# Moving the last conditioning product into the entry of the feed-forward part, with results added by transfer and forms made later

## The chip, the cores and the metric

The kernel runs as one program on one core of a Trainium2 chip. The metric is the device time of one execution in microseconds. A matrix product on TensorE (PE in the profile) has a stationary operand, loaded by a weight load (PEld), and a moving one, whose columns stream through it; the result lands in PSUM, in banks of 512 fp32 columns by 128 partitions. VectorE (DVE) and ScalarE (ACT) read PSUM and work on SBUF, GpSimd (POOL) issues transfers of its own kind, and SyncE's queue (SP) issues the weight loads from HBM.

## What is computed

One decoder layer for 512 prompt rows and 8 sample rows (520 columns, with features on the partitions). Cut to what matters here:

```python
sh1, sc1, g1, sh2, sc2, g2 = ada_mod(c, w_ada, b_ada)     # six conditioning parts, each 2048 wide
...
merged = sigmoid(ga) * (y_m @ w_proj_a) + sigmoid(gb) * (y_f @ w_proj_b)
x = x + g1 * (merged @ w_out)
h2 = modulate(rmsnorm(x, norm2_w), sh2, sc2)
a, g = split(h2 @ w_ffn_in)                               # 2 x 5632 wide
f_out = (gelu(conv3(a) + conv_b) * g) @ w_ffn_out
x = x + g2 * f_out
```

`ada_mod` multiplies nine conditioning vectors (one of the prompt, eight of the samples) by `w_ada`, 2048 by 6 x 2048. So each of the six parts is a product with only nine rows of use, but 16.8 MB of weights. `g2`, the last of them, is needed only when `w_ffn_out` is multiplied.

## The kernel before, in words

**Products.** All large products keep fp32 accuracy with rounded operands: a weight is split into a rounded high part `wh` (a copy on ScalarE) and the rest `wl` (a subtraction on VectorE), as is the input, and each 128 x 128 block takes three matmuls, wh·xh, wh·xl and wl·xh (`three_of`). A matmul has 260 columns, half of the 520.

**Pairs.** From `w_out` on, two output rows of blocks at a time go through one step of Strassen's scheme: seven products instead of eight (`class Pair`, L256). A unit has seven products of 24 matmuls, numbered 1 to 7, in `ORDER` = (1,5,6,3,7,2,4), or for the first unit of a part `ORDER1` = (1,2,3,5,6,7,4) (L254). They go to the PSUM tiles `x` (products 1, 6, 7, 4), `y` (5, 3) and `z` (2). Product n needs its weights summed (`total`, tiles `sw`) and split (`split`), and the forms of the input `X[n]` (sums of the input's four quarters, each split in high and low part). `run_pairs` (L337) writes the order of work out by time steps t: at each step it finishes the product before (`take`), prepares weights two steps ahead (`ahead`), runs what the dictionary `late` holds for t, and issues product t.

**Order.** From L1139 to L1147 and from L1661 on, TensorE, VectorE and ScalarE keep the order in which the program lists their instructions (`Ordered`, L53). Weight tiles `raw` are 128 x 1024 (512 KB), in eight buffers (L157 to L163); SP issues their loads in program order, each as soon as a buffer is free.

**Conditioning.** `ada_mm` (L418) multiplies one block of 128 rows of `w_ada`: the stationary operand is `cs`, 128 x 32 (nine columns of use), and the 2048 outputs are four groups of 512 columns that go to four groups of 32 columns of the array (`tile_position=(0, 32*g)`), and so to four groups of 32 partitions of one bank `adp`. The operands are plain fp32, and each such matmul runs in two passes. The parts SC2 and SH2 are 18 steps (`ada_steps`, L503: eight of two blocks each and a last one, for each part) that `due` (L192) takes from a list at every `calls[2]`-th call. A dense product over 16 blocks calls `due` twice, one over eight blocks once. `calls` is (0, 1, 3) over the 16 dense products of the FoX projections (L1275), 1 of 5 over the last five gate products (L1444), and 1 of 2 over the products with `w_pb` (L1449). The part G2 has its own functions (L2104 to L2127): from the fourth unit of the feed-forward pairs on, one block is loaded into four `ar` tiles (`g2_load`) and multiplied before a product 2 (`g2_product`), 16 times, every second unit; then come a copy to SBUF, four transposes and the bias.

**The products with `w_pb`** (L1598 to L1636). 16 products over eight blocks. Product n of the loop has output block j of `order` = 0, 8, 1, 9, ..., 7, 15. It is multiplied by its gate in `mg[j]`, then the branch of `w_pa`, which lies in HBM (`dmg`) and was loaded into `mgo` by SP, is added on VectorE. Right after, `m_first` (j < 8) makes form 1 or `m_forms` makes the other six forms of blocks j-8 and j. Forms 6 and 4 of the blocks 0 to 6 go to HBM and are fetched back by POOL.

**The entry of the feed-forward part** (L1821 to L1884). The input `h2` comes half by half (`features`, VectorE and ScalarE, with the tiles `xa` and `bf`), and meanwhile the first three output blocks f = 0, 1, 2 are multiplied without Strassen's scheme, `eight(f, o, e, zs, w)`: eight blocks of K, one or two halves z, 24 matmuls for each half (`beside` takes two such sets side by side). Their PSUM tiles are `acc[f][o][z]`. For f = 1 these are four banks of their own, `fb`, of which 260 of 512 columns are used. `sums_of` and `sum_parts` make the forms for the pairs, `whole_conv` and `whole_gate` finish a block. The last set, `eight(2, 1, 1)`, is issued at step -2 of the pairs (L2136), and steps -1 to 3 hold what is left of the entry on VectorE.

Of the kernel before, what the change touches and what calls it, by code (L numbers as in the profile page):

```python
# [63 lines left out]
def tile_hybrid_step(ctx: ExitStack, tc: tile.TileContext, I, O):  # L64
# [28 lines left out]
    def pt(name, dt=F32):  # L93
        return sp.tile([P, 528], dt, tag="p", name=nm(name), bufs=8)
# [1177 lines left out]
        return t  # L1272

    pending += ada_steps(SC2) + ada_steps(SH2)
    calls[:] = 0, 1, 3  # L1275

    dqf = dram([2, NS, 4 * P], "dqf")
    sc = mconst([P, NPG, NS, FH], "sc")
# [190 lines left out]
    def m_forms(i):  # L1469

        a, b = mg[i], mg[8 + i]
        mX[2][i], mX[3][i] = hl_parts(hp, "hl", b)
        b11, b12, b21, b22 = (t[:, o:o + HN] for t in (a, b) for o in (0, HN))
        V.tensor_tensor(b11, b11, b12, op=ALU.subtract)
        V.tensor_tensor(b12, b22, b12, op=ALU.subtract)
        V.scalar_tensor_tensor(b22, b22, -1.0, b11, op0=ALU.mult, op1=ALU.subtract)
        V.scalar_tensor_tensor(b21, b22, -1.0, b21, op0=ALU.mult, op1=ALU.subtract)
        mX[5][i], mX[7][i] = hl_parts(hp, "hl", a)
        for n, f in ((6, b22), (4, b21)):
            t = (st if i == 7 else pt)("mf", F32R)  # L1480
            hi, lo = mX[n][i] = parts_of(t)
            S.copy(hi, f)
            V.tensor_tensor(lo, f, hi.bitcast(F32), op=ALU.subtract)
            if i < 7:
                G.dma_start(dxf[i + 8 * (n == 4)][:, :N], t[:, :N])
        mg[i] = mg[8 + i] = None
# [52 lines left out]
    class WoPair(AddPair):  # L1539
# [45 lines left out]
        def end(self, step):  # L1585

            if step == 0:
                self.add(1, 0, self.x)
            if step == 1:
                super().c11()  # L1590
                self.done(0)
                self.done(1)

# [3 lines left out]
    for n, j in enumerate(order):  # L1597
# [16 lines left out]
            units[0].load((1, 0), (1, 1))  # L1614
        if n % 2 == 0 and n // 2 + 2 < NB2:
            fetch_gate(n // 2 + 2)
        old = pt("mgo")
        nc.sync.dma_start(old[:, :N], dmg[j])
        acc = dense(I["w_pb"][j], yf, "pb", raw=early.pop(j, None))
        if n == KC - 1:  # L1620
            more.append(cf)
# [8 lines left out]
        V.tensor_tensor(mg[j][:, :N], mg[j][:, :N], old[:, :N], op=ALU.add)  # L1630
        if j < 8:
            m_first(j)
        else:
            m_forms(j - 8)
    yf = old = None

    def shift(c):
# [18 lines left out]
    def parts2(u, o, e):  # L1656
        return wtwo([raws.pop((u, o, e))], 1024)
# [34 lines left out]
    def first_weights(o):  # L1692
# [2 lines left out]

    r2 = st("rr")
    run_pairs(units, 2, {
        9: log_exp, 50: lambda: fetch_xa(range(8)), 51: lambda: (load2(0, 0, 0), load2(0, 1, 0)), 53: tot_parts,
        54: lambda: (first_weights(0), half_squares(1)), 55: lambda: (first_weights(1), half_norm(1))}, 0)
    mX = units = None  # L1700

# [73 lines left out]
    done = []  # L1775
    part = {}

    def whole_conv(f):
        at = new_at()
        for z in range(2):  # L1780
            S.copy(at[:, 2 + z * HN:2 + (z + 1) * HN], acc[f][0][z])
        acc[f][0] = None
        part[f] = conv_start(f, at)
        conv_end(f, at, part[f])

# [18 lines left out]
    def sum_parts(n):  # L1804
        src = [{5: xa[i][:, :HN], 7: xa[i][:, HN:N], 4: xa[8 + i][:, :HN], 6: xa[8 + i][:, HN:N]}[n] for i in range(8)]
        for j in range(8 + 1):
# [7 lines left out]
            if j >= 1:  # L1814
# [3 lines left out]
                else:  # L1818
                    V.tensor_tensor(lo, src[j - 1], hi.bitcast(F32), op=ALU.subtract)

    features(0, 1, {0: lambda: W2.end(0), 2: lambda: W2.end(1), 3: lambda: half_squares(0), 6: lambda: ws.append(parts2(1, 0, 0))})  # L1821
    load2(0, 0, 1)
    some = [(0, 0, ws[0]), (0, 1, ws[1])]
    beside(some, 0, 1, range(4))
    half_norm(0)
    acc.append([[mm_ps("fb")[:, :HN] for z in range(2)] for o in range(2)])
# [12 lines left out]
    for e in range(2):  # L1839
# [27 lines left out]
    eight(2, 1, 0, (1, 0), w0)  # L1867
    for i in range(8):
        hb.pop((i, 1))
    w = parts2(1, 1, 1)  # L1870
# [6 lines left out]
    for i in range(6, 8):  # L1877
        sums_of(i)
    eight(2, 0, 1, (0, 1), w0)
    w = parts2(2, 1, 1)  # L1880
    sum_parts(5)
    whole_gate(1)
# [216 lines left out]
        return late  # L2099


    box = {}

    def g2_load(k):  # L2104
        box["raw"] = [pt("ar") for _ in range(4)]
        for g, t in enumerate(box["raw"]):
            nc.sync.dma_start(t[:, :512], I["w_ada"][k * P:(k + 1) * P, G2 * DM + g * 512:G2 * DM + (g + 1) * 512])

    def g2_product(k):
        if k == 0:  # L2110
            box["ps"] = mm_ps("adp")
        ada_mm(box["ps"], [(k, t[:, :512], k == 0, k == KC - 1) for t in box.pop("raw")], False)

    def g2_out():
        box["sb"] = pt("ads")
        S.copy(box["sb"][:, :512], box.pop("ps"))

    def g2_turn():
        t = ada_turn(box.pop("sb"), 4)
        c0 = G2 * 16  # L2120
        dst = ada[:, c0:c0 + 16, :].rearrange("p (g j) i -> p j g i", g=4)
        bias = wide(C_ADA + c0, 16).rearrange("p (g j) i -> p j g i", g=4)
        for j in range(4):
            V.tensor_tensor(dst[:, j], t[:, j, :, :9], bias[:, j], op=ALU.add)
        negative(G2)

    g2 = {}  # L2127
    for k in range(KC):
        g2.update({7 * (4 + 2 * k) + 2: on(g2_load, k), 7 * (4 + 2 * k) + 5: on(g2_product, k)})
    g2.update({7 * 36: g2_out, 7 * 36 + 2: g2_turn})  # L2130
# [111 lines left out]
```

## Time and profile before

| | |
|---|---|
| median of 3 runs | 2923.01 us (2921.05 to 2929.48) |
| the profiled execution | 2912.86 us |
| its span, first to last instruction | 2911.2 us |
| mean granted TensorE clock | 0.997 |

The profile is of one execution. Times in its rows are microseconds from the start of the span. PE's rows give a modelled duration that is longer than the distance between the starts of two matmuls, since they overlap; the distance is what a matmul costs in a full stream. DMA share is the mean busy share of the core's 16 DMA engines. A row of the timeline merges instructions alike that follow each other; xN is their number, and what stands in brackets is the engine's idle time before, and what ended it.

### The profile page before, as it was taken

The numbers are of one execution on the slowest core, as the hardware profiler recorded it, in microseconds if no ns is written. First come the engines' busy times: TensorE is split into PE (matmuls) and PEld (weight loads), VectorE is DVE, ScalarE is ACT, GpSimd is POOL, SyncE is SP. The second block draws the span as 40 slices with busy tenths as digits, with TensorE's granted clock in tenths as the row PEclk, the third lists the DMA queues.
The fourth block names the chain that finished last, engine by engine and source line by source line (L and its number), as shares of the span: only waits on it lengthen the run. The fifth ranks groups of instructions, "written<-read, shape, count | busy, mean of one in ns | idle before, by whom it ended". The sixth has DMA issues, their size and how long they took to land. (4 is left out here: it accounts for less than half of the span.)

```text
span 2911.2 us, 58503 instructions
## 1 busy us (share of the span) xinstructions
PE 2853.6 (98%) x23460; PEld 2730.7 (94%) x23460; DVE 2176.0 (75%) x3984; ACT 1341.4 (46%) x2321; POOL 419.6 (14%) x681
## 2 busy tenths in 40 slices
PE   6999999999999999999999999999999999999999
PEld 4889998999999889889999999999999999999999
DVE  4777875577864567358888888888888888787787
ACT  3234433355544545334555544444444445544543
POOL 0003430211110122501111100000000001100100
PEclk9999999999999999999999999999999999999999
DMA  9933437845445555787672344344434436746752
GB/s 338 305 115 114 149 125 268 293 153 168 146 152 172 196 176 189 247 302 247 208 245 73 122 137 153 126 148 136 154 128 146 138 124 182 193 157 188 203 160 89
DMA packets 214138, 514.16 MB, mean 177 GB/s; under 512 B 24481, under 2 KB 77073, under 8 KB 213865
## 3 DMA queue, kind: packets, MB, share of 16 engines
q1 hardware_dynamic: 177072, 416.01, 43.9%
q0 software_dynamic: 36352, 94.18, 10.7%
q8 instruction: 184, 3.01, 0.4%
q14 instruction: 90, 0.73, 0.1%
q10 hardware_dynamic: 440, 0.23, 0.0%
HBM read 440.40 MB, written 66.46 MB: 174 GB/s over the span
## 5 line engine op out<-in xcount | busy, mean ns | idle before, releaser
L60 ACT CAST wh<-sw 128x512 fp32r<-128x512 f32 x640 | 366.7, 621 | 244.9 <-PE z L60 87.2
L60 PE MATMUL x<-bf,wh 128*128 128x260 f32 x2624 | 476.9, 283 | 1.0 <-DVE tg L60 0.5
L60 DVE TENSOR_TENSOR wl<-sw,wh 128x512 fp32r<-128x512 f32 x640 | 412.3, 686 | 83.2 <-ACT wh L60 80.3
L60 DVE TENSOR_TENSOR wl<-raw,wh 128x1024 fp32r<-128x1024 f32 (+2 forms) x325 | 337.7, 1051 | 121.2 <-ACT wh L60 115.2
L60 ACT CAST wh<-raw 128x1024 fp32r<-128x1024 f32 (+2 forms) x325 | 292.0, 912 | 268.6 <-PE x L60 122.7
L60 PEld LDWEIGHTS x<-bf,wh 128*128 128x128 f32 x2624 | 404.1, 188 | 1.4 <-DVE tg L60 0.7
L60 PE MATMUL x<-bf,wl 128*128 128x260 f32 x1312 | 369.8, 282 | 0.0
L178 DVE TENSOR_TENSOR wl<-raw,wh 128x1024 fp32r<-128x1024 f32 (+1 forms) x140 | 171.5, 1226 | 194.5 <-ACT wh L177 180.9
L177 ACT CAST wh<-raw 128x1024 fp32r<-128x1024 f32 (+1 forms) x140 | 144.1, 1031 | 285.1 <-issue 50.5
L60 PEld LDWEIGHTS x<-bf,wl 128*128 128x128 f32 x1312 | 246.6, 188 | 0.0
L60 PE MATMUL y<-bf,wh 128*128 128x260 f32 x1312 | 239.2, 283 | 2.9 <-ACT wh L60 2.4
L60 PEld LDWEIGHTS y<-bf,wh 128*128 128x128 f32 x1312 | 201.4, 188 | 3.3 <-ACT wh L60 2.6
L60 DVE TENSOR_TENSOR sw<-raw,raw 128x512 f32<-128x512 f32 x316 | 203.1, 683 | 0.0
L60 PE MATMUL x<-ff,wh 128*128 128x260 f32 x1024 | 186.3, 283 | 0.0
L60 PE MATMUL y<-bf,wl 128*128 128x260 f32 x656 | 185.0, 282 | 0.2 <-DVE wl L60 0.2
L60 PEld LDWEIGHTS x<-ff,wh 128*128 128x128 f32 x1024 | 157.9, 188 | 0.0
L60 PE MATMUL x<-ff,wl 128*128 128x260 f32 x512 | 144.6, 282 | 0.0
L60 PE MATMUL x<-hf,wh 128*128 128x260 f32 x720 | 131.6, 282 | 1.0 <-ACT wh L60 0.6
L60 PE MATMUL fo<-fe,wh 128*128 128x260 f32 x768 | 125.4, 284 | 1.1 <-DVE fo L60 0.9
L60 PEld LDWEIGHTS y<-bf,wl 128*128 128x128 f32 x656 | 123.4, 188 | 0.4 <-DVE wl L60 0.4
L60 PE MATMUL z<-bf,wh 128*128 128x260 f32 x656 | 121.6, 286 | 0.0
L60 PEld LDWEIGHTS z<-bf,wh 128*128 128x128 f32 x656 | 100.8, 188 | 13.4 <-issue 13.4
(597 smaller groups left out, 7607.0 us busy)
## 6 DMA issues: line engine op xcount, KB each, us to landing
raw<-in_w_fi SPq DMA_DIRECT2D x176, 512.0 KB
raw<-in_w_in SPq DMA_DIRECT2D x156, 512.0 KB
ar<-in_w_ada SPq DMA_DIRECT2D x192, 256.0 KB
raw<-in_w_ada SPq DMA_DIRECT2D x96, 512.0 KB
raw<-in_w_fo SPq DMA_DIRECT2D x64, 512.0 KB
raw<-in_w_out SPq DMA_DIRECT2D x32, 512.0 KB
raw<-in_w_fo SPq DMA_DIRECT2D x32, 384.0 KB
dff<-cc POOLq DMA_DIRECT2D x44, 260.0 KB
```

The costliest lines, as they stand in the source:

```text
L60: return lambda *a, **k: self.tc.keep_in_program_order(getattr(self.eng, op)(*a, **k))
L177: S.copy(wh[:, o], t[:, :m])
L178: V.tensor_tensor(wl[:, o], t[:, :m], wh[:, o].bitcast(F32), op=ALU.subtract)
```

## The change

1. `calls` over the FoX projections is (0, 1, 2) in place of (0, 1, 3): a step of SC2 and SH2 at every second call.
2. In the loop over `w_pb`, for the first 14 products the branch of `w_pa` is no longer loaded by SP and added by VectorE: POOL issues a transfer from HBM that adds it to `mg[j]`. The last two keep the old way. The forms of product n are made at the end of product n+1. At the end of the last one stand `m_first(7)` and the first part of `m_forms(7)`, now called `m_second`; the rest of `m_forms(7)` comes at step 0 of the pairs with `w_out`.
3. The tiles x, y and z of the last `w_out` unit are let go at its end.
4. G2 moves from the pairs into the entry. Its eight double steps (two blocks each, loaded as four `raw` tiles of 512 KB) stand between the sets of the entry. Its four groups of 512 columns are cut in three pieces of 252, 252 and 8 columns, which go to the spare columns 260 to 511 of three of the four `fb` banks. A group's three pieces follow each other. The copy to SBUF takes three instructions; transposes, bias and `negative` (`g2_turn`) stand after `eight(2, 0, 1)`.
5. At the start of the pairs, `whole_conv(2)` is split: its copies from PSUM stay at step -1, the rest goes to step 1; `sum_parts(7)` moves from step -1 to 2, `whole_gate(2)` from 0 to 3, `sum_parts(4)` from 3 to 4.

```diff
-    calls[:] = 0, 1, 3
+    calls[:] = 0, 1, 2
...
-        old = pt("mgo")
-        nc.sync.dma_start(old[:, :N], dmg[j])
+        if n >= KC - 2:
+            old = pt("mgo")
+            nc.sync.dma_start(old[:, :N], dmg[j])
...
-        V.tensor_tensor(mg[j][:, :N], mg[j][:, :N], old[:, :N], op=ALU.add)
-        if j < 8:
-            m_first(j)
+        if n < KC - 2:
+            G.dma_start(mg[j][:, :N], dmg[j], accum_op=ALU.add)
         else:
-            m_forms(j - 8)
+            V.tensor_tensor(mg[j][:, :N], mg[j][:, :N], old[:, :N], op=ALU.add)
+        for i in order[n - 1:n] + order[n:] * (n == KC - 1):
+            if i < 8:
+                m_first(i)
+            elif i < KC - 1:
+                m_forms(i - 8)
+            else:
+                m_second(7)
...
+    def g2_load(k):
+        box["raw"] = [[wraw(I["w_ada"][i * P:(i + 1) * P, G2 * DM + e * 1024:G2 * DM + (e + 1) * 1024])
+                       for e in range(2)] for i in (k, k + 1)]
+
+    def g2_room():
+        (_, a), (b, c) = fbt[1], fbt[0]
+        return [(c, 0, 252), (b, 252, 504), (a, 504, 512)]
+
+    def g2_product(k):
+        for i, t in zip((k, k + 1), box.pop("raw")):
+            for g in range(4):
+                for bank, a, b in g2_room():
+                    T.matmul(bank[32 * g:32 * g + 32, HN:HN + b - a], cs[:, i, :],
+                             t[g // 2][:, g % 2 * 512 + a:g % 2 * 512 + b], start=False, stop=(i == KC - 1),
+                             tile_position=(0, 32 * g), skip_group_check=True)
+        if k < KC - 2:
+            g2_load(k + 2)
...
     beside(some, 0, 0)
+    g2_load(0)
     eight(1, 0, 0, (0,), ws[2])
...
     eight(1, 1, 0, (1, 0), w)
+    g2_product(0)
...
     features(1, 1, {3: lambda: some.append((0, 1, parts2(0, 1, 1)))})
     load2(2, 0, 0)
+    g2_product(2)
     beside(some, 1, 1)
...
     features(1, 0)
+    g2_product(4)
     beside(some, 1, 0)
+    g2_product(6)
...
     whole_conv(0)
     w0 = parts2(2, 0, 0)
     load2(1, 1, 1)
+    g2_product(8)
     eight(1, 0, 1, (0, 1), w)
...
+    g2_product(10)
     eight(2, 0, 0, (1, 0), w0)
...
+    g2_product(12)
     eight(2, 1, 0, (1, 0), w0)
+    g2_product(14)
+    g2_out()
...
     eight(2, 0, 1, (0, 1), w0)
+    g2_turn()
     w = parts2(2, 1, 1)
     sum_parts(5)
     whole_gate(1)
...
-    run_pairs(units, 2, {-2: lambda: eight(2, 1, 1, (0, 1), w), -1: lambda: (whole_conv(2), sum_parts(7)),
-                         0: lambda: whole_gate(2), 3: lambda: sum_parts(4),
-                         **g2, **whole[0].begin(7 * len(units))})
+    run_pairs(units, 2, {-2: lambda: eight(2, 1, 1, (0, 1), w), -1: lambda: whole_copy(2),
+                         1: lambda: whole_conv(2), 2: lambda: sum_parts(7), 3: lambda: whole_gate(2),
+                         4: lambda: sum_parts(4),
+                         **whole[0].begin(7 * len(units))})
```

More of the change, by code (lines that the diff above doesn't have):

```diff
@@ L1467, in m_first, with m_second, m_forms @@
         V.tensor_tensor(lo, a[:, :HN], hi.bitcast(F32), op=ALU.subtract)
-    def m_forms(i):
+    def m_second(i):
+        mX[2][i], mX[3][i] = hl_parts(hp, "hl", mg[8 + i])
+    def m_forms(i, second=True):
         a, b = mg[i], mg[8 + i]
-        mX[2][i], mX[3][i] = hl_parts(hp, "hl", b)
+        if second:
+            m_second(i)
         b11, b12, b21, b22 = (t[:, o:o + HN] for t in (a, b) for o in (0, HN))
@@ L1590, in end @@
                 super().c11()
+                self.x = self.y = self.z = None
                 self.done(0)
@@ L1697, in tile_hybrid_step @@
     run_pairs(units, 2, {
-        9: log_exp, 50: lambda: fetch_xa(range(8)), 51: lambda: (load2(0, 0, 0), load2(0, 1, 0)), 53: tot_parts,
+        0: lambda: m_forms(7, False), 9: log_exp, 50: lambda: fetch_xa(range(8)), 51: lambda: (load2(0, 0, 0), load2(0, 1, 0)), 53: tot_parts,
         54: lambda: (first_weights(0), half_squares(1)), 55: lambda: (first_weights(1), half_norm(1))}, 0)
@@ L1776, in tile_hybrid_step, with whole_copy @@
     part = {}
-    def whole_conv(f):
-        at = new_at()
+    def whole_copy(f):
+        part[f] = at = new_at()
         for z in range(2):
@@ L1782, in whole_conv @@
         acc[f][0] = None
+    def whole_conv(f):
+        if f not in part:
+            whole_copy(f)
+        at = part[f]
         part[f] = conv_start(f, at)
@@ L1819, in sum_parts, with g2_out, g2_turn @@
                     V.tensor_tensor(lo, src[j - 1], hi.bitcast(F32), op=ALU.subtract)
+    box = {}
+    def g2_load(k):
[13 more added lines that the diff above has]
+            g2_load(k + 2)
+    def g2_out():
+        box["sb"] = pt("ads")
+        for bank, a, b in g2_room():
+            S.copy(box["sb"][:, a:b], bank[:, HN:HN + b - a])
+    def g2_turn():
+        t = ada_turn(box.pop("sb"), 4)
+        c0 = G2 * 16
+        dst = ada[:, c0:c0 + 16, :].rearrange("p (g j) i -> p j g i", g=4)
+        bias = wide(C_ADA + c0, 16).rearrange("p (g j) i -> p j g i", g=4)
+        for j in range(4):
+            V.tensor_tensor(dst[:, j], t[:, j, :, :9], bias[:, j], op=ALU.add)
+        negative(G2)
     features(0, 1, {0: lambda: W2.end(0), 2: lambda: W2.end(1), 3: lambda: half_squares(0), 6: lambda: ws.append(parts2(1, 0, 0))})
@@ L1825, in tile_hybrid_step @@
     half_norm(0)
-    acc.append([[mm_ps("fb")[:, :HN] for z in range(2)] for o in range(2)])
+    fbt = [[mm_ps("fb") for z in range(2)] for o in range(2)]
+    acc.append([[t[:, :HN] for t in ts] for ts in fbt])
     beside(some, 0, 1, range(4, 8))
@@ L1866, in tile_hybrid_step @@
         sums_of(i)
+    g2_product(12)
     eight(2, 1, 0, (1, 0), w0)
+    g2_product(14)
+    g2_out()
+    fbt = None
     for i in range(8):
@@ L2099, in rest_of @@
         return late
[L2102 to L2130, printed above, removed]
     units = [FfnPair(f, ORDER1 if f == 3 else ORDER) for f in range(3, KF)]
```

## The prediction

> **What bounds the kernel.** First the page: TensorE is busy for 98% of the span, at full clock nearly everywhere.
>
> ```profile
> span 2911.2 us, 58503 instructions
> PE 2853.6 (98%) x23460; PEld 2730.7 (94%) x23460; DVE 2176.0 (75%) x3984; ACT 1341.4 (46%) x2321; POOL 419.6 (14%) x681
> ```
>
> So the change can only win where PE waits, or where work leaves PE. Second, the chain in order of time, in the pairs, where the G2 product (`adp`) is now:
>
> ```profile
> 1653.83 2.89 PE z L60 x24
> ...
> 1673.94 2.88 PE z L60 x24
> ...
> 1694.07 0.99 PE adp L60 x8
> 1695.06 3.07 PE z L60 x24
> ...
> 1715.37 2.89 PE z L60 x24
> ```
>
> The chain runs on PE alone. A product takes 2.88 us for 24 matmuls, 0.12 each. A unit without G2 takes 1673.94 - 1653.83 = 20.11; the next two units take 1715.37 - 1673.94 = 41.43, not 40.22. One G2 block thus costs 1.21 (0.99, and the rest around it), and its 16 blocks 16 x 1.21 = **19.4 us**, uncovered.
>
> Third, the stretches around the entry, cut where sets of products begin. (Columns: length, busy time of PE, PEld, DVE, ACT, POOL, granted clock, DMA share, GB/s.)
>
> ```profile
> 1519.30:1526.10 6.80, 6.18 (x25) 5.79 (x25) 5.26 (x12) 3.71 (x8) 2.04 (x6) 0.50 0.73 270
> 1551.70:1553.60 1.90, 0.90 (x5) 0.50 (x4) 1.90 (x7) 1.31 (x3) 0.00 (x0) 1.00 0.37 65
> 1553.60:1593.60 40.00, 40.00 (x335) 40.00 (x335) 37.17 (x80) 23.63 (x48) 7.99 (x11) 1.00 0.26 91
> 1593.60:1616.20 22.60, 18.53 (x147) 17.50 (x146) 22.27 (x46) 11.25 (x25) 5.90 (x7) 1.00 0.33 106
> ```
>
> The entry is nearly as tight on VectorE (37.17 of 40, then 22.27 of 22.6) as on PE. PE loses about 1.5 us in the second row, where it waits for features. In the last row it does six products, 17.3 us of work, in 22.5: 5.2 lost. About 1.9 of those are three places where one tile is used by two products in a row (3 then 5, 6 then 7, 7 then 4, some 0.63 each); 3.3 are VectorE being late. DMA is light, 91 GB/s.
>
> **Part by part.**
>
> *G2 out of the pairs:* -19.4, worked out above. The four transposes cost the same 0.5 in either place.
>
> *G2 in the entry.* The trace has the same double step, with 512 columns whole, for another conditioning part:
>
> ```profile
> 436.45 0.40 PE L223 MATMUL gate<-hh,wl 128*128 128x260 f32 x2
> 436.79 1.92 PE L421 MATMUL adp<-raw,cs 128*32 128x512 f32 x16
> 438.64 0.51 PE L223 MATMUL gate<-hh,wh 128*128 128x260 f32 x2
> 438.99 0.40 PE L223 MATMUL gate<-hl,wh 128*128 128x260 f32 x2
> ```
>
> From 436.45 to 438.99 less four ordinary matmuls (0.48) is 2.06 us for two blocks, against 2.42 for two single ones: each return to full-width matmuls costs some 0.36. Eight double steps are 16.5; two pairs of them (0 and 2, 6 and 8) stand with no product between, so -0.7. The pieces of 8 columns add 2 passes in each of 16 blocks, four groups abreast: 32 passes that the trace doesn't show, between 0 and the 0.12 of a 260-column matmul, 0 to 3.8. I take 0.04 (far nearer to empty), 1.3. Sum **+17.1**, if the four groups still run abreast. That is the open point (first two rows: `adp`'s instructions alone that lie in a stretch of 0.03 us, on PE, PEld and ACT):
>
> ```profile
> 1693.99:1694.02 0.03, 0.02 (x4) 0.03 (x4) 0.00 (x0) 1.00 1.01 416
> 1694.44:1694.48 0.04, 0.04 (x8) 0.00 (x0) 0.00 (x0) 1.00 0.50 208
> 1694.00 1.06 PE L60 MATMUL adp<-ar,cs 128*32 128x512 f32 x8
> L60 PE MATMUL adp<-ar,cs x128: 592/605/617, 1694.0 to 2315.8; 128*32 128x512 f32 x128
> ```
>
> Four passes begin within 0.03 us, one of each group, and the second four about 0.45 later: eight passes of 0.6 each end within 1.06. The program lists a group's two passes one after the other, so a group doesn't hold up the next one for at least one waiting pass. After the change five passes of group 0 are listed ahead of group 1. If they hold it up, a block takes four times one group's time: 4 x (4 passes of 252 columns at 0.215 + 2 x 0.04) = 3.8 instead of about 1.0, **+45** over 16 blocks. Between "abreast" and that lies everything; I take abreast, since every group of passes seen overlaps fully.
>
> The Trainium skill ("TensorE: Matmul & The Clock Gate", Part 3) says that matmuls start and end strictly in program order. By that rule the +45 would hold. The rows above contradict it for the passes, as the second pass of one group starts after the first of the next, but they can't exclude it for whole matmuls. The same page gives the queue 64 entries; the 36 weight loads and passes listed ahead of the last group would fit.
>
> *Its loads.* G2 adds 32 loads of 512 KB to the eight `raw` buffers. SP is already waiting for free buffers there:
>
> ```profile
> SPq L163 <- DVE wl L60: 32.6, 5, 14.2
> 1240.00:1310.00 70.00, 70.00 (x582) 61.69 (x575) 40.63 (x72) 21.40 (x36) 4.32 (x8) 1.00 0.90 312
> ```
>
> The second row shows what the transfers can give: 312 GB/s at a share of 0.90, so 347. Counting buffers in program order, the loads for steps 0 and 2 are in before PE reaches them at 1551.7. All later ones wait for buffers that step 0 frees. From its half to the second half of step 8 there are 15 loads (12 of G2, 3 of `w_fi`), 7.9 MB or 22.7 us, and I add 2 from issue to first bytes (an estimate, 0 to 4). PE's own work in that time is two sets of 5.8 and 4 double steps, 19.6. So PE waits **+5.1** (3 to 7), most of it at steps 4 and 8, which have nothing or one set in front. If the groups run one after the other this wait vanishes. Behind the waiting step on PE stand the entry's sets, and what VectorE makes from them.
>
> *What it covers:* the 1.5 us of waiting for features, **-1.5**.
>
> *The new tie of VectorE to PE.* `g2_turn` puts four VectorE additions, in program order, ahead of the last weights' split and of `sum_parts(5)`; they read transposes that follow `eight(2, 0, 1)` on PE. Until now VectorE ran ahead here:
>
> ```profile
> 1584.02 1.22 DVE L60 TENSOR_TENSOR wl<-raw,wh 128x1024 fp32r<-128x1024 f32 x1
> 1585.15 2.80 DVE L60 TENSOR_TENSOR bf<-xa,bf 128x260 fp32r<-128x260 f32 x8
> 1587.87 0.75 DVE L60 TENSOR_TENSOR cc<-fb,cc 128x260 f32<-128x260 f32 x2
> 1588.54 2.79 DVE L60 SCALAR_TENSOR_TENSOR bf<-xa,bf 128x260 fp32r<-128x260 f32 x8
> 1591.26 1.28 DVE L60 TENSOR_TENSOR sw<-raw,raw 128x512 f32<-128x512 f32 x2
> 1592.46 1.21 DVE L60 TENSOR_TENSOR wl<-raw,wh 128x1024 fp32r<-128x1024 f32 x1
> 1593.60 1.28 DVE L60 TENSOR_TENSOR sw<-sw,raw 128x512 f32<-128x512 f32 x2
> L60 DVE TENSOR_TENSOR ada<-adq,sv x4: 179/180/185, 2350.4 to 2350.7; 128x36 f32<-128x36 f32 x4
> ```
>
> `eight(2, 1, 1)` is the last 5.8 us before 1593.6, so PE ended `eight(2, 0, 1)` at about 1587.8; the split (first row) was done by 1585.2. Now VectorE can begin only when the transposes are through: four additions of 0.18, the negation, 1.22 for the split, about 2.3 us in which PE has two matmuls to do: wait 2.3. From the split's end VectorE needs 1593.60 - 1585.15 = 8.45 until product 1 has its weights; PE has 5.5: wait 3.0. Moving `whole_conv(2)` and `sum_parts(7)` behind then lets products 2, 3 and 5 go through, but the same VectorE work remains before product 4 and the next unit: 1.3 more, and the 1.9 of the tile uses. Together 8.5 in place of 5.2, **+3.3** (0 to +6). The lead that VectorE gains while PE does G2 is lost at this tie.
>
> *Waits and the clock.* A lowered clock cost 3.4 us once (first stretch row: 6.8 us at 0.50). The 2.4 us wait for product 3 (1593.60:1616.20) left it at 1.00. So I take 0, and 3.4 more as the upper end. The Trainium skill ("TensorE: Matmul & The Clock Gate", Part 1) has the clock halve after an idle window of about 3.4 us; by that rule a wait of 3.0 could do it or not, which would add the same 3.4.
>
> *Results added by transfer, forms later.* VectorE drops 14 additions:
>
> ```profile
> L1630 DVE TENSOR_TENSOR sgm<-sgm,mgo x16: 690/700/701, 1253.4 to 1350.9; 128x520 f32<-128x520 f32 x16
> L1563 POOL DMA_DIRECT2D tot<-sq x13: 887/902/964, 1376.9 to 1499.7; - x13
> 1355.19 0.28 PE L60 MATMUL z<-mf,wl 128*128 128x260 f32 x1
> 1356.65 0.51 PE L60 MATMUL y<-mf,wh 128*128 128x260 f32 x2 [1.19 <-ACT wh L60]
> ```
>
> That is 9.8 us, but VectorE is busy for only 40.6 of 70 us there (row 1240:1310), so it is worth nothing in the loop. POOL's adding transfers take about 0.9 to issue and have a whole product, 5.8 us, to land before the form reads `mg[j]`; they cover themselves. At the end of the loop the order changes: product 3 of `w_out` waited 1.35 us (last two rows) behind `m_forms(7)`; now that comes after its weights, but before product 5's, and one more form (of block 6) has slid to the last product. What product 5 waits on is nearly the same sum. I take **-0.7** (-2 to +1). Letting x, y, z go earlier: nothing waits on them. The rate of SC2 and SH2: 32 calls at 1 of 2 make 16 steps instead of 10, and the last 2 of 18 follow in the gates, so none is left for the `w_pb` loop. The same steps at 2.06 us cost PE the same earlier; the loop's DMA share of 0.90 shows that PE (70.00 of 70) bears a denser stream: 0 (-1 to +2).
>
> **Sum:** -19.4 + 17.1 + 5.1 - 1.5 + 3.3 - 0.7 = **+3.9** on the profiled execution, 2912.9 to 2916.8. That execution is 10 us below the median of the three runs, 2923.0; on the median's scale, 2927.
>
> **Rivals.**
>
> *A, groups one after the other* (slower). Place: `g2_product`. Price: +45, less the load waits of 5.1, so +44 in all: 2967. It decides from the point where the queue in front of a group's passes holds fewer than the five that the others must jump. For it: the order of the program; against: the rows at 1694. A milder form, in which a group starts when the one before is half through, gives about 2.2 a block: +20 - 5 + 4 = +19, 2942.
>
> *B, PE fills VectorE's gaps* (faster). If buffers come free sooner than I count (no load waits) and VectorE catches up after its tie (no loss at the boundary): 3.9 - 5.1 - 3.3 = -4.5, 2918.5; with the lowered clock at 1519 gone as well, -8, 2915. For it: PE gets 17 us more work in the entry, in which VectorE's stays the same. Against: VectorE's order is fixed.
>
> *C, the change doesn't do what it says:* the forms spread nothing, since the last product now carries three of them: product 5 waits 1 to 2 us longer, 2929. Inside the range.
>
> **Chances.** Forecast (abreast, loads and tie as priced) 0.5, with a range of its own of 2919 to 2935; A's mild form 0.2, A in full 0.17; B 0.13. The range leaves out the lower part of B and the upper part of A: 2917 to 2964. A measurement of this kernel can tell about 0.3% (8.8 us) from no change. Faster by that needs more than all of B: 0.06. Within it: most of B and about seven tenths of the forecast, 0.43. Slower: A and the rest, 0.51.
>
> **What would show it.** The `adp` passes' place: one double step of about 2.2 us (abreast) or 7 (one after another) between sets. PE waiting on `raw` from `w_ada` before steps 4 and 8. VectorE idle until the transposes, then PE waiting for `wl` at `eight(2, 1, 1)` and product 1. A unit of the pairs at 20.11 throughout. The forecast is wrong if G2's passes take much over 1.1 us a block, or if PE's waits between the entry and the steady pairs come to less than 8 or more than 20.

## The result, and the profile after

The changed kernel is slower: 2968.2 us median (2964.5 to 2971.4, four runs) against 2922.0 (2920.6 to 2929.5) before, a ratio of 1.0154 (95% interval 1.0138 to 1.0170). The profiled execution took 2964.5 us, 51.6 more than that of before. The page of the changed kernel begins so:

```profile
span 2962.8 us, 58873 instructions
...
PE 2882.9 (97%) x23716; PEld 2763.4 (93%) x23716; DVE 2166.8 (73%) x3970; ACT 1340.6 (45%) x2323; POOL 423.1 (14%) x695
```

TensorE is busy 29 us longer, and the span is 52 us longer: so part is work (or slower work), part is waiting. Where it lies is seen when both traces are cut at the same matmuls. First before, then after, in four stretches: the FoX projections (first to last matmul on `fi`), the products with `w_pb`, from their end to the first matmul of the entry (the pairs with `w_out`), and the entry. (Columns: length, busy time of PE, PEld, DVE, ACT, POOL, granted clock, DMA share, GB/s.)

```profile
868.90:1126.20 257.30, 254.24 (x2021) 230.62 (x2021) 150.53 (x343) 128.66 (x250) 43.16 (x42) 1.00 0.54 182
...
1246.75:1349.42 102.67, 102.67 (x853) 94.81 (x852) 71.18 (x122) 35.88 (x55) 8.07 (x16) 1.00 0.83 284
1349.42:1517.39 167.97, 163.70 (x1353) 162.34 (x1352) 140.98 (x269) 90.86 (x150) 33.97 (x54) 1.00 0.75 233
1517.39:1593.54 76.15, 74.25 (x581) 72.86 (x582) 65.21 (x144) 43.54 (x84) 13.32 (x29) 0.96 0.32 108
```

```profile
870.32:1133.74 263.42, 263.42 (x2127) 233.96 (x2127) 151.86 (x346) 129.66 (x252) 43.02 (x44) 1.00 0.67 227
...
1256.20:1370.33 114.13, 100.22 (x769) 97.14 (x768) 52.48 (x87) 31.03 (x49) 19.87 (x27) 0.96 0.59 155
1370.33:1546.81 176.48, 167.29 (x1354) 165.49 (x1352) 148.53 (x283) 93.59 (x156) 34.87 (x56) 0.98 0.73 223
1546.81:1661.12 114.31, 109.26 (x970) 95.68 (x970) 63.17 (x145) 40.77 (x79) 10.48 (x29) 0.97 0.63 219
```

| stretch | before | after | difference |
|---|---|---|---|
| FoX projections | 257.3 | 263.4 | +6.1 |
| from there to the first product with `w_pb` | 120.6 | 122.5 | +1.9 |
| products with `w_pb` | 102.7 | 114.1 | +11.5 |
| pairs with `w_out`, up to the entry | 168.0 | 176.5 | +8.5 |
| entry | 76.2 | 114.3 | +38.2 |
| from its last matmul to product 2 of the second unit of the pairs | 40.0 | 42.9 | +2.9 |
| pairs, from there to the end | 809.8 | 789.2 | -20.7 |
| product with `w_ffn_out`, first to last matmul on `fo` | 302.5 | 304.4 | +1.9 |

Look at the second row of each fence. Before, PE is busy for all of 102.67 us, and six conditioning steps (five of two blocks and a short last one) are among its work. After, these are gone (853 matmuls become 769), and yet the stretch is longer: PE is idle for 13.9 us, the clock is lowered, and VectorE has less to do (52.5 for 71.2). Two places that the prediction had at nothing or at half, the loop and the entry, hold the loss. The pairs gave what was expected: a unit now takes the same time throughout (three starts of `z`, in the chain):

```profile
1724.27 2.88 PE z L60 x24
...
1744.37 2.88 PE z L60 x24
...
1764.48 2.86 PE z L60 x24
```

**The loop over `w_pb`, after.** The timeline, its rows on other work left out:

```profile
1285.12 0.69 DVE L1635 TENSOR_TENSOR sgm<-pb,sgm 128x520 f32<-128x520 f32 x1
...
1286.11 0.90 POOL L1637 DMA_DIRECT2D sgm<-dmg  x1 [5.66 <-DVE sgm L1635]
...
1290.36 1.16 ACT L1459 CAST mf<-sgm 128x520 fp32r<-128x520 f32 x2 [5.14 <-DMA sgm<-dmg]
...
1290.38 0.43 DVE L1479 TENSOR_TENSOR sgm<-sgm,sgm 128x260 f32<-128x260 f32 x1 [3.44 <-DMA sgm<-dmg]
...
1291.43 1.05 ACT L177 CAST wh<-raw 128x1024 fp32r<-128x1024 f32 x1
...
1293.06 0.69 DVE L1635 TENSOR_TENSOR sgm<-pb,sgm 128x520 f32<-128x520 f32 x1
...
1293.89 0.47 PE L223 MATMUL pb<-yfh,wh 128*128 128x260 f32 x2 [1.36 <-DVE sgm L1635]
```

A product is multiplied by its gate (1285.12), POOL issues the adding transfer (1286.11), and 4.25 us later it has landed. In the program the forms that read it stand behind the next multiplication. On VectorE's queue they stand ahead of it: this loop doesn't lie in one of the stretches where the program's order is kept. So VectorE waits 3.44 us for the transfer, the next multiplication comes only at 1293.06, the PSUM tile is not free, and PE waits. ScalarE's copy of the next weights (1291.43) stands behind a form too. In sums, over 1280 to 1400 (total, times, longest):

```profile
ACT mf L1459 <- DMA sgm<-dmg: 35.8, 6, 8.3
...
DVE sgm L1479 <- DMA sgm<-dmg: 25.6, 6, 6.6
...
PE pb L223 <- DVE sgm L1635: 10.1, 7, 4.0
```

**The entry, after.** One double step of G2, and all of G2 in the entry:

```profile
1612.76 0.28 PE L60 MATMUL fb<-bf,wl 128*128 128x260 f32 x1
1612.97 4.26 PE L60 MATMUL fb<-raw,cs 128*32 128x252 f32 x48
1617.16 0.51 PE L60 MATMUL fa<-bf,wh 128*128 128x260 f32 x2
```

```profile
L60 PE MATMUL fb<-raw,cs 128*32 128x252 f32 (+1 forms) x384 | 33.5, 313 | 0.2 <-DMA raw<-in_w_ada 0.2
```

From the start of the last matmul ahead to that of the first behind, less one ordinary matmul, a step of two blocks takes 1617.16 - 1612.76 - 0.12 = 4.28 us, not 2.06; the eight, taken likewise, 33.8 without the wait behind the last. PE waits only 0.2 us for G2's loads. Two ties follow, the first on ScalarE (`ads` is G2's copy from PSUM, at 1637), the second on VectorE (`adq`, at 1653); behind each stand the waits of PE:

```profile
1637.09 0.83 ACT L60 COPY ads<-fb 128x252 f32<-128x252 f32 x3 [32.44 <-PE fb L60]
...
1638.90 1.23 DVE L60 TENSOR_TENSOR wl<-raw,wh 128x1024 fp32r<-128x1024 f32 x1 [27.50 <-ACT wh L60]
...
1638.92 0.51 PE L60 MATMUL fb<-bf,wh 128*128 128x260 f32 x2 [1.43 <-ACT wh L60]
...
1640.18 0.39 PE L60 MATMUL fb<-bf,wl 128*128 128x260 f32 x1 [0.75 <-DVE wl L60]
...
1653.71 0.50 DVE L60 TENSOR_TENSOR ada<-adq,sv 128x36 f32<-128x36 f32 x4 [2.92 <-PE adq L60]
...
1655.61 0.39 PE L60 MATMUL fg<-bf,wl 128*128 128x260 f32 x1 [1.69 <-DVE wl L60]
...
1664.05 0.39 PE L60 MATMUL x<-bf,wl 128*128 128x260 f32 x1 [2.41 <-DVE wl L60]
```

**The clock.** Between the start of the FoX projections and the last product it was lowered once, for 6.8 us, before, and ten times, for 3.4 us each, after, five of them between 1310 and 1392.

### The profile page after: what moved, and what is told of

It is laid out like the page before. It is cut to its first block, busy times and chain, and to the rows that moved or that the text cites. A ratio compares the mean times of both kernels' runs of the same rounds, so it can differ in the third digit from the quotient of the medians.

```text
span 2962.8 us, 58873 instructions
## 1 busy us (share of the span) xinstructions
PE 2882.9 (97%) x23716; PEld 2763.4 (93%) x23716; DVE 2166.8 (73%) x3970; ACT 1340.6 (45%) x2323; POOL 423.1 (14%) x695
## 3 DMA queue, kind: packets, MB, share of 16 engines
q0 software_dynamic: 38368, 97.91, 11.5%
## 4 chain that ended last, share of the span: by engine, by line
PE 87%; DVE 4%; issue 3%; DMA 2%; ACT 1%; POOL 1%; SPq 0%; POOLq 0%; ACTq 0%; DVEq 0%
PE x L60 31%; PE y L60 15%; PE z L60 8%; PE fi L223 6%; PE gate L223 4%; PE fo L60 4%; PE pa L223 3%; PE pre L609 3%; PE adp L421 2%; PE mo L223 2%; PE fb L60 2%; PE mv L223 2%; PE fa L60 1%; DMA sgm<-dmg 1%; DVE wl L60 1%
## 5 line engine op out<-in xcount | busy, mean ns | idle before, releaser
L60 PEld LDWEIGHTS x<-hf,wh 128*128 128x128 f32 x720 | 111.0, 188 | 1.4 <-ACT wh L60 0.7
```

The lines of the kernel that those rows point to most:

```text
L60: return lambda *a, **k: self.tc.keep_in_program_order(getattr(self.eng, op)(*a, **k))
```

## The experiments

All ratios are to the kernel before, run on the same chip in turn; in brackets the 95% interval. Two things about comparing. The profiled execution of before, 2912.9 us, is below every other run of that kernel (2915.9 to 2932.4); between 1126 and the first product with `w_pb` even kernels with the same instructions there took 120 to 135 us. So stretches are compared by traces, and whole kernels by ratios.

### One part alone

**e1, the transfers and later forms alone.** In the kernel before, part 2 of the change:

```diff
-        V.tensor_tensor(mg[j][:, :N], mg[j][:, :N], old[:, :N], op=ALU.add)
+        if n < KC - 2:
+            G.dma_start(mg[j][:, :N], dmg[j], accum_op=ALU.add)
```

> The kernel before with only the branch of w_pa added by transfer and the forms made a product later (part 2 of the change); conditioning rate and G2 as before. Theory Q (a queue): VectorE's and ScalarE's queues hold the forms of product n-1 ahead of the multiplication or the weights of the next product, and the forms wait some 4 us for the transfer that has just been issued, so that TensorE waits for PSUM or weights. The changed kernel reached the entry 29.4 us later than before, about 27 of it by this. Here six conditioning steps (12.4 us of TensorE work) stay in the loop and may hide a part: 15 to 30 us slower, 2937 to 2952. Rival R (the rate and its loads, or the longer stretch ahead, made the loop late): the transfer is covered by a product of 5.8 us, as the prediction said, so within 3 us of before, 2919 to 2925.

Measured: 1.0105 (1.0088 to 1.0122), 30.7 us by the ratio, 2957.1 median. The stretch over `w_pb` takes 121.0 us (102.7 before), that of `w_out` 177.5 (168.0). So the transfers lose 27.8 us by themselves, at the upper end of what was expected; the rate isn't needed for it.

**e2, G2 in the entry alone.** Parts 3, 4 and 5; the core:

```diff
+    g2_product(0)
...
-    g2.update({7 * 36: g2_out, 7 * 36 + 2: g2_turn})
```

> The kernel before with only G2 in the entry, in three pieces per group, with its out-copies and turn, and the split steps at the start of the pairs (parts 3, 4, 5); the loop over w_pb as before. From the marks of the two traces: entry +38, boundary +3, pairs -21, end +2. Theory: these stand by themselves, so 18 to 24 us slower, 2940 to 2946. Rival: a part of the entry's +38 is the delay of the features or transfers left over from the disturbed loop ahead; then 5 to 15 slower, 2927 to 2937. What the prediction said of this part alone (-19.4 + 17.1 + 5.1 - 1.5 + 3.3 = +4.6): 2927.

Measured: 1.0082 (1.0061 to 1.0102), 24 us, 2951.1 median. The entry takes 114.0 us, as in the whole change (114.3), although nothing is disturbed ahead of it. The loss is the entry's own.

**e3, the change without its transfers.** The old load and addition for all 16 products:

```diff
-        if n < KC - 2:
-            G.dma_start(mg[j][:, :N], dmg[j], accum_op=ALU.add)
-        else:
-            V.tensor_tensor(mg[j][:, :N], mg[j][:, :N], old[:, :N], op=ALU.add)
+        V.tensor_tensor(mg[j][:, :N], mg[j][:, :N], old[:, :N], op=ALU.add)
```

> The changed kernel with the branch of w_pa loaded by SP and added by VectorE again for all 16 products; the forms are still made a product later, the rate and G2 stay changed. Theory Q: the wait for the transfer was the loss, so the time before the entry comes back but for a few us: 24 to 30 faster than the changed kernel, 2938 to 2944. Rival R (rate or deferral made the loop late): within 5 us of 2968.

Measured: 1.0042 (1.0027 to 1.0057), 2940.8 median. The two stretches, `w_pb` and `w_out`:

```profile
1258.15:1349.97 91.82, 91.82 (x769) 91.82 (x768) 70.13 (x115) 35.49 (x54) 7.38 (x14) 1.00 0.57 183
1349.97:1518.20 168.23, 163.40 (x1353) 162.25 (x1352) 140.75 (x268) 90.71 (x150) 34.78 (x56) 1.00 0.77 235
```

PE is busy for all of the first. Against the changed kernel that is 22.3 us and 8.3 us: **the transfers cost 30.6 us**, and rival R is out.

### What about the transfer costs

**e4, forms held behind the next multiplication.** Order of issue alone:

```diff
+        for i in order[n - 2:n - 1] if n > 1 else []:
+            with tc.issue_after(seen["mult"].ins), tc.issue_after(seen["wh"].ins):
+                m_first(i) if i < 8 else m_forms(i - 8)
```

> The changed kernel with the transfers kept, but the forms of product n-1 held in VectorE's queue behind the multiplication of product n and in ScalarE's queue behind the weights of product n+1 (order of issue alone). Theory Q: the transfer of about 4 us then lies beside a whole product and the loss goes: 20 to 30 faster than the changed kernel, 2938 to 2948. Rival T (the transfers themselves cost: their traffic, or the result that lands late): within 5 us of 2968.

Measured: 1.0094 (1.0071 to 1.0116), 2956.9 median. That is some 17 us less than the changed kernel by the ratios, less than theory Q asked for.

```profile
1264.02:1363.01 98.99, 94.89 (x770) 93.77 (x768) 52.90 (x86) 29.84 (x48) 21.56 (x30) 0.98 0.70 181
1363.01:1539.15 176.14, 167.69 (x1353) 165.49 (x1352) 148.70 (x283) 94.12 (x156) 33.31 (x53) 0.98 0.73 222
```

The loop came down by 15.1 of its 22.3; the 8 us at `w_out` stayed. POOL's rows and ScalarE's in this run point to the reason:

```profile
1299.24 1.20 POOL L1489 DMA_DIRECT2D dxf<-mf  x2 [4.38 <-DVE mf L1487]
1300.49 0.89 POOL L1640 DMA_DIRECT2D sgm<-dmg  x1
...
1307.63 0.63 ACT L1459 CAST mf<-sgm 128x520 fp32r<-128x520 f32 x1 [7.56 <-DMA sgm<-dmg]
```

POOL issues an adding transfer behind two stores of forms, which had to wait for VectorE; two stores and two transfers then move in one queue, 1065 KB from 1300.4 to 1309.5, and the copy to a form that needs the transfer begins 7.1 us after the issue at 1300.49. As we read it, the forms are late, so the multiplication behind them is late, so the next transfer is late: the lag carries itself.

**e9, the traffic without anybody waiting.** On the version with rate and later forms (e6, below):

```diff
+            V.tensor_copy(spare[n % 3][:, :1], mg[j][:, :1])
+            G.dma_start(spare[n % 3][:, :N], dmg[j], accum_op=ALU.add)
```

> The version with the rate changed and the forms a product later, G2 in the pairs (0.9972 of before), to which 14 adding transfers of the same size are added that read the same rows of HBM and add them to spare tiles, each issued right after its product's multiplication; nothing reads the spare tiles, and they are no part of the result. Theory Q (someone waits for the landing): the stretch from the first to the last product with w_pb stays at 92 us, the stretch to the entry at 167 to 168, in all 0.996 to 0.999 of before. Rival T (the transfers' traffic or POOL's time costs): a good part of the 30 us comes with them, over 1.004.

Measured: 0.9968 (0.9957 to 0.9979), 2913.2 median, like e6 without this traffic (0.9972).

```profile
1256.89:1348.72 91.83, 91.83 (x770) 91.83 (x769) 70.72 (x129) 35.39 (x54) 20.31 (x28) 1.00 0.82 224
```

The DMA share rises from 0.57 to 0.82, POOL's time from 7.4 to 20.3, and PE loses nothing. The transfers cost nothing; waiting for them does.

**e10, forms two products later.** As e4, but the three lines stand behind the multiplication of product n; G2 in the pairs.

```diff
         seen["mult"] = V.tensor_tensor(z2(mg[j]), acc, z2(mg[j]), op=ALU.mult)
...
+        for i in order[n - 2:n - 1] if n > 1 else []:
+            with tc.issue_after(seen["mult"].ins), tc.issue_after(seen["wh"].ins):
```

> The rate changed, the branch of w_pa added by transfer, G2 in the pairs; the forms of product n-2 stand in VectorE's queue behind the multiplication of product n and in ScalarE's behind the weights of product n, a product later than in the run that held them. Theory L (what holding left over is the length of the transfer: two adding transfers and two stores of forms, 1065 KB, lay together in POOL's queue for 7 to 9 us): now a transfer has about 11.6 us, and the stretch over w_pb takes 92 to 94 us where the held version took 99 and the changed kernel 114. Rival: VectorE's or ScalarE's queue is still what is late; then 97 or more. At the start of w_out more forms come late in either case.

Measured: 0.9994 (0.9979 to 1.0009), 2921.4 median.

```profile
1257.97:1352.76 94.79, 92.87 (x769) 92.05 (x768) 54.07 (x87) 31.26 (x50) 20.36 (x28) 1.00 0.70 182
1352.76:1526.12 173.36, 165.83 (x1353) 163.87 (x1352) 147.12 (x283) 92.33 (x154) 34.57 (x56) 0.99 0.75 229
```

The loop is within 3 us of the 91.8 without transfers (0.8 us over the expected range). So of the 22.3, 15.1 came back with the place in the queue and 4.2 more once a transfer had a product longer to land (some 1.7 of these 4.2 are the clock, which was at half for 3.4 us in the loop of e4 and stayed up in this one). The other 3.0 are left; ScalarE still waits for transfers here, five times and 30.8 us in all. `w_out` still loses 5.1; three products' forms now come after the last one, which may be the reason.

**e11, transfers for the first eight products only.**

```diff
-        if n < KC - 2:
+        if n < 8:
             G.dma_start(mg[j][:, :N], dmg[j], accum_op=ALU.add)
```

> The rate changed, forms a product later, G2 in the pairs; only the first 8 of the 16 products have their branch added by transfer, the others by load and VectorE. Theory: the loss in the loop goes with the number of transfers (22 us for 14, so 10 to 14 for 8: a stretch of 102 to 106 us), and the 8 us lost at the start of w_out come from the backlog that VectorE and ScalarE carry out of the loop, so they vanish (167 to 169). Rival: the start of w_out loses 8 us whichever products had transfers, since the later forms alone cause it; 175 or more.

Measured: 1.0012 (0.9999 to 1.0025), 2925.9 median.

```profile
1259.60:1369.27 109.67, 99.87 (x769) 98.02 (x768) 64.37 (x107) 34.33 (x54) 14.92 (x23) 0.94 0.56 160
1369.27:1536.52 167.25, 163.09 (x1354) 162.14 (x1352) 140.59 (x268) 90.60 (x150) 34.37 (x55) 1.00 0.77 236
```

The second row settles the 8 us at `w_out`: they vanish when the loop's last products have no transfer. So it was the backlog carried out of the loop, not the later forms. The first row missed: eight transfers cost 17.9 us, not 10 to 14. The clock was down for 13.7 us of this stretch (0.94), half of which, 6.8, is lost; why it was down longer here than with 14 transfers (10.2 us) isn't shown.

### The rate, and the forms made later

**e5, the rate alone.**

```diff
-    calls[:] = 0, 1, 3
+    calls[:] = 0, 1, 2
```

> The kernel before with only the rate of the conditioning steps changed (one at every second call of the FoX projections). Theory as in the prediction: the same steps cost the same earlier, so within 4 us of before: 2924 to 2932 on the scale of a before at 2928. Rival G (a gain): the changed kernel without its transfers was only 12 us over before although the G2 move alone cost 23, so 10 to 11 came from the rate or from the later forms; if from the rate, 2916 to 2919.

Measured: 0.9954 (0.9940 to 0.9968), 2910.3 median against 2921.1. **This is the lowest ratio of all**, 13 us under the kernel before (9 to 18); the intervals of e6 and e9 overlap with it. The FoX projections and the loop:

```profile
869.87:1133.30 263.43, 263.43 (x2128) 233.97 (x2127) 151.77 (x346) 129.55 (x252) 43.00 (x44) 1.00 0.68 227
...
1262.35:1354.17 91.82, 91.82 (x769) 91.82 (x768) 70.54 (x115) 35.50 (x54) 8.34 (x16) 1.00 0.60 190
```

Six more double steps, 12.4 us at 2.06 each, lengthen the FoX projections by only 6.1 us. The 3.06 us in which PE was idle there are filled, which is half of the difference; the other half isn't placed. Five fewer, and the short last one, shorten the loop by 10.85. One step fewer between these stretches is worth some 2 more. That makes 7; the measured gain is 9 to 18. What the rest is, the stretch between, which scatters by 15 us from run to run, doesn't let us say.

**e6, rate and later forms.** e5, and the forms of product n at the end of product n+1:

```diff
-        if j < 8:
-            m_first(j)
-        else:
-            m_forms(j - 8)
+        for i in order[n - 1:n] + order[n:] * (n == KC - 1):
```

> The kernel before with the rate changed and the forms of the loop over w_pb made a product later; the branch of w_pa still loaded and added by VectorE, G2 in the pairs. Theory: the difference of the two earlier runs, 12 minus 23, holds by itself, so 8 to 12 faster than before, 2916 to 2920 on the scale of a before at 2928. Rival: the gain is one that only the moved G2 leaves room for; then within 3 of before.

Measured: 0.9972 (0.9959 to 0.9984), 2913.1 median. The stretch of `w_out` takes 167.3, against 168.2 with the rate alone. That 1 us is no more than the scatter: the stretch took 167.3 to 168.7 in the four traces with later forms and no transfer (e3, e6, e9 without a reader of its transfers, e12), and 168.0 to 168.9 in the five with forms made at once (before, e2, e5, e7, e8). What the later forms are worth isn't shown; the gain is the rate's.

### G2

**e7, groups inside, pieces outside.** e2, with

```diff
-            for g in range(4):
-                for bank, a, b in g2_room():
+            for bank, a, b in g2_room():
+                for g in range(4):
```

> As the run with G2 alone in the entry, but the four groups of a piece follow each other (piece outside, group inside) instead of the three pieces of a group. Theory D (a short window): the next group's first pass could start only when no more than three passes waited ahead, so a block took 1.82 us, two groups at a time; now a block takes 1.0 to 1.1, 16 blocks gain 11 to 13: 2938 to 2941 where G2 alone took 2951. Rival: a block costs 1.8 by its weight loads and passes of 252 and 8 columns whatever their order: 2949 to 2953.

Measured: 1.0063 (1.0046 to 1.0080), 2938.2 median against 2921.1; that is 5.6 us less than e2 by the ratios, whose intervals overlap (the entry of the traces is 7.4 us shorter, 106.5 for 114.0), not 11 to 13. But a double step (its rows, then the waits of PE's weight loads and of its matmuls in the entry):

```profile
1589.87 0.28 PE L60 MATMUL fb<-bf,wl 128*128 128x260 f32 x1
1590.08 2.01 PE L60 MATMUL fb<-raw,cs 128*32 128x252 f32 x48
1592.02 0.51 PE L60 MATMUL fa<-bf,wh 128*128 128x260 f32 x2
```

```profile
PEld fb L60 <- DMA raw<-in_w_ada: 8.5, 7, 2.3
PE fb L60 <- DMA raw<-in_w_ada: 6.2, 7, 2.2
```

takes 2.03 us in place of 4.28, as theory D said. What passes begin first shows it directly. In the first 0.86 us of a step of the changed kernel, before any piece of 8 columns, and in its first 0.43 us:

```profile
L60 PE MATMUL fb<-raw,cs x6: 376/376/400, 1613.0 to 1613.7; 128*32 128x252 f32 x6
...
L60 PE MATMUL fb<-raw,cs x2: 376/388/400, 1613.0 to 1613.2; 128*32 128x252 f32 x2
```

and in the first 0.23 us here:

```profile
L60 PE MATMUL fb<-raw,cs x4: 400/400/400, 1590.1 to 1590.1; 128*32 128x252 f32 x4
```

In the changed kernel one group runs alone for 0.43 us: two passes begin, and nothing beside them. Of the six, four are group 0's two long pieces; the other two are group 1's. So the next group begins together with the third pass of the group before, when three of that group's six are still to begin: 8 groups x 0.455 us, the longer last group and the change of width make 4.28. Here four groups begin at once. Of the 8 x 2.25 = 18 us thus won the entry keeps 7.4: now that PE is quicker, it waits 6.2 us (its weight loads 8.5) for G2's loads.

**e8, besides, the two ties undone.**

```diff
-    g2_out()
-    fbt = None
...
     w0 = parts2(2, 0, 1)
+    g2_out()
+    fbt = None
...
-    g2_turn()
...
-                         4: lambda: sum_parts(4),
+                         4: lambda: sum_parts(4), 9: g2_turn,
```

> As the run before it, and besides the copies of G2 from PSUM stand behind the copies of the next weights and whole_conv(1) on ScalarE, and the transposes and additions (g2_turn) in the second unit of the pairs. Theory: the two ties (VectorE idle 27 us, then 3 us; TensorE waiting about 8 us with the lowered clock) cost 4 to 9 us: 2930 to 2936. Rival: VectorE's and ScalarE's work in the entry is the bound at this place, ties or not: within 2 us of the run before it.

Measured: 1.0037 (1.0025 to 1.0050), 2932.1 median, 6 us less than e7. The ties were worth about what the rows of PE's waits behind them say (1.43, 0.75, 1.69 and 2.41, together 6.3).

**e12, the change mended:** e3 with the edits of e7 and e8.

```diff
-            G.dma_start(mg[j][:, :N], dmg[j], accum_op=ALU.add)
...
+            for bank, a, b in g2_room():
+                for g in range(4):
...
+                         4: lambda: sum_parts(4), 9: g2_turn,
```

> The whole change but for three places: the branch of w_pa is loaded by SP and added by VectorE for all 16 products; in G2 the piece is outside and the group inside; out-copies and turn of G2 stand later. If the parts add up (the rate and later forms 0.9954 to 0.9972, G2 abreast and untied 1.0037): 0.999 to 1.001 of before. Rival: the entry's waits for G2's loads and the earlier conditioning steps disturb each other; 1.003 or more.

Measured: 0.9986 (0.9976 to 0.9996), 2917.3 median against 2922.9, just under what was expected. The parts add up. G2 in the entry still doesn't pay: the entry takes 99.4 us where e6 has 75.1, +24.3, the stretch behind it costs 1.5 more, the pairs give 20.6. The version to keep is e5, the rate alone.

## Why the prediction was wrong, step by step

It said 2927 (2917 to 2964); the time is 2968. That this lies near the upper end is chance: that end stood for rival A, whose milder form came true and by itself would have given 2942; the rest of the loss comes from terms that had nothing to do with it. The steps in its order:

- **G2 out of the pairs, -19.4: right.** From the second unit to the end of the pairs the difference is -20.7, in e2 -19.5. Units are 20.1 us apart throughout.
- **G2 in the entry, four groups abreast, +17.1: wrong**; its milder rival A was right. The eight steps took 33.8, 2.1 us a block, where that rival had 2.2; over 1.1 a block was its own sign of being wrong. The rows at 1694 showed a group jumping over one waiting pass and were stretched to five. In e7, where they do run abreast, a step costs 2.03: the 2.06 and the small price of the 8-column pieces were sound.
- The Trainium skill ("TensorE: Matmul & The Clock Gate", Part 3) has matmuls start and end strictly in program order. Neither that nor "abreast" held: six long passes began before group 0's short piece, which the program lists fifth and sixth, so two of group 1's passed it; yet only one group could be ahead.
- **Waits for G2's loads, +5.1: as it said for either case.** It said that they vanish if the groups run one after the other: 0.2 us. Abreast PE's are 6.2 (3 to 7 was the range), all but 0.4 of it at steps 4 and 8, where it put most of them.
- **The wait for features, -1.5: right.** In the changed kernel PE waits for no feature after the entry's first 3 us, and between there and 1637 for G2's loads alone, 0.2 us.
- **VectorE's new tie, +3.3: right in size**, with the waits of 1.69 and 2.41 us that it placed at `eight(2, 1, 1)` and product 1. The first of them lies in the entry. Behind the entry the table has +2.9, but 1.4 of that isn't the tie's: 40.0 us for that stretch is low, and five of the six other traces with G2 in the pairs have 41.3 to 41.5, with the clock at half for 3.4 us. That leaves 1.7 + 1.5 = 3.2. With the turn made later (e8) the stretch still takes 42.9 (44.2 in e7); a wait of some 3 us ahead of product 5 is left. **Its twin was missed:** `g2_out` puts three copies ahead of ScalarE's next weights in program order, so ScalarE waited 32.4 us for G2's last pass, VectorE 27.5 behind it, and PE 2.2. The gain of e8 is both.
- **The clock, 0, at most 3.4: wrong.** It went down ten times for 3.4 us instead of once for 6.8; at half clock that is 17 us in place of 3.4, some of it in time that PE waited anyway.
- **Results added by transfer, forms later, -0.7: this step failed most.** "They cover themselves", it said, since a transfer has a whole product to land. That took the program's order for the queue's. In this loop instructions are put in another order, and the forms went ahead of the next multiplication. With the loop at 22.3 and the backlog at `w_out` 8.3 it cost 30.6 us. Its other half, the later forms alone (-2 to +1), was not contradicted: at `w_out` they make no difference clear of the scatter (e6), and the 1 to 2 us more of rival C aren't seen there.
- **The rate, 0 (-1 to +2): wrong the other way.** "The same steps cost PE the same earlier" left out the idle 3.06 us of the FoX projections, where six steps cost 6.1 in place of 12.4. By traces -7, by the ratio -13 (-9 to -18).

The errors have both signs: +31 by the transfers, +17 by the slow groups, -5 by the load waits that these made vanish, +4 by the tie of ScalarE (2.2 and the clock behind it, 1.7), -7 to -13 by the rate. That is +34 to +40, and with the +4 forecast 38 to 44, where 46 was measured; the 2 to 8 us left over aren't placed.

## What to carry to other kernels

When a result is handed to a transfer, look up what stands behind its first reader on each engine's real queue, not in the program, and count from the issue to the landing, with what shares the issuer's queue. Order matmuls for different column groups so that neighbours in the list belong to different groups; a list that stays long in one group runs nearly alone. Look for stages where TensorE is idle before moving work: there it is cheap, and a stage with no idle time gives its full price back.

## What the runs showed of the hardware

**Short waits can lower the clock for 3.4 us.** Four stretches of the changed kernel, in the order of time (the seventh column from the left, after the five busy times, is the clock):

```profile
1292.99:1296.40 3.41, 2.18 (x16) 2.00 (x17) 2.57 (x5) 0.54 (x2) 1.78 (x3) 1.00 0.29 18
1296.40:1303.20 6.80, 6.36 (x52) 5.97 (x51) 2.60 (x4) 1.36 (x2) 1.12 (x2) 1.00 0.87 234
...
1306.66:1310.07 3.41, 1.65 (x12) 1.27 (x11) 3.38 (x7) 1.34 (x3) 0.89 (x1) 1.00 0.02 5
1310.07:1313.48 3.41, 3.41 (x18) 3.41 (x18) 0.21 (x1) 0.44 (x2) 1.12 (x2) 0.50 0.94 181
```

With PE idle for 1.23 of 3.41 us the clock stayed up in the next stretch; with 1.76 idle it went to half. The Trainium skill ("TensorE: Matmul & The Clock Gate", Part 1) has the clock halve after an idle window of about 3.4 us. Here no wait in the loop so far was longer than 1.5 us, so less than a full idle window is enough. The other traces narrow it down. In each of the 14, all changes of the clock lie whole multiples of 3.413 us apart. Cut into stretches of that length, from 60 us on, each stretch at full clock in which PE was idle for over 1.82 us was followed by one at half, and none with less than 1.11 us idle was; in between both occur. What decides there, these runs don't say.

**Column groups don't run abreast from any distance in the list:** with six passes listed per group a new group began every 0.455 us, with two listed all four began within 0.03 us. An 8-column pass adds about 0.03 us.

**An adding transfer of 260 KB** has landed 4.25 us after its issue when alone in POOL's queue, and 7.1 us after it beside two stores and a second transfer (one case each, by the start of the instruction that waited for it).
